# Last projection of a hybrid decoder block by seven products, with earlier x^T quarter loads, an ACT-freed retention bank and an earlier gated split

## The chip, the cores and the metric

One Trainium2 chip, one of its cores. The metric is device microseconds of one execution of the whole kernel (all of its inputs in HBM, the output written back to HBM). Its engines each run their own instructions in order: TensorE (PE, with its weight loads as PEld), VectorE (DVE), ScalarE (ACT), GpSimd (POOL) and SyncE (SP, which here only issues DMAs). Waits between engines are semaphores.

## The reference

One decoder layer on x of 512 tokens by 1024 channels, all in float32:

```
h = rms_norm(x, norm_pre);  proj = h @ w_in           # w_in: 1024 x 6936
o_a = nsa(...)        # compressed, selected and sliding-window attention, 8 heads
y_a = (o_a * silu(z_n)) @ w_nsa_o
o_b = retention(...)  # 4 heads, chunks of 128 tokens, group norm
y_b = (o_b * silu(z_r)) @ w_ret_o
merged = sigmoid(m_a) * y_a + sigmoid(m_b) * y_b
out = x + rms_norm(merged @ w_out, norm_post)         # w_out: 1024 x 1024
```

## The kernel before, in words

Every float32 product is made of three: each operand is split into a high part (rounded to the fp32r type, whose products PE takes at full rate) and a low part (the rest), and high x high, low x high and high x low are added up in a PSUM bank of 128 x 512. All matmuls go through `mm` (L230). The split of an operand is a copy for the high part, mostly by ACT (`act`, L197), and a subtraction for the low part by DVE (`sub_split`, which ends in `tt`, L209).

**Weights** come as a stream of 512 KB pieces. `load_next` (L356 for the plain ones, L359 for DRAM tiles) has SP load one into `raw` (4 buffers); each is split in two halves into `whi`/`wlo` (9 buffers each). One such half is the right-hand side or the weights of one k-tile. A buffer of `raw` is free when both halves are split, one of `whi`/`wlo` when PE has used it.

**The order of PE's work** is `main` (L1385) with the table `PLAN`: attention projections, then Z, MA 0, ZR 0, QK 0, VR 0, ZR 1, QK 1, VR 1, MB 0, NO 0, RO 0, MA 1, NO 1, MB 1, RO 1, and last `merged @ w_out`. Attention and retention are threaded between them. The program is written as coroutines; a planner (class `Order`) runs them at build time with a cost for each instruction and so fixes the order on every engine. A coroutine's priority is the second argument of `od.spawn` (a smaller number first), and `yield r, "act"` means "not before r, and when ACT's queue is short". What the planner thinks of time appears nowhere in this text; what matters is that each engine's order is fixed, so that an instruction that waits holds up all behind it.

**Seven products.** MA 1 and MB 1 already use a Winograd form: a 1024 x 512 projection is cut in quarters, and seven products of quarters stand in for eight (`seven`, L1219). Sums of weight quarters are made by DMAs in DRAM, issued by POOL: copies (L336) and accumulating DMAs (L338), all while attention runs (`weight_sums`). Sums of quarters of h^T are made by `h_sums`/`h_sum` (L1161, L1173): x^T is loaded again, scaled on ACT, added on DVE, split into the tiles `sums`.

**Places the change touches.**
- `ret` (L1013) ends a VR tile: ACT writes the high part of V from the bank, then DVE reads the same bank for the low part (`stt`, L222); only then is the accumulation bank free. PE's products go alternately to two such banks (`ACC`).
- `ret` also takes a reciprocal square root on POOL (`rv`, L209), for which DVE waits.
- `ga_split` (L1293) splits the gated attention output when all of retention is done; NO 0 needs it.
- `h_sums` waits for the same, then loads x^T; `tail_ya` (L1304) multiplies a bank of NO by its gate on DVE and frees the bank.
- `tail_yb` (L1311) ends a bank of RO: gate, sum with the NO part, split into `MO_H`/`MO_L`, the merged operand of the last projection.
- The last projection: two halves of 512 output channels, four token tiles t each, 8 k-tiles, three matmuls each. The last tile is done as two of 256 columns:

```
for half in range(2):
    for t in range(NT):
        n = 256 if half and t == NT - 1 else 512
        for j in range(512 // n):
            ps, e = yield from nat(...)          # 8 k-tiles x 3 matmuls of n columns
            od.spawn(tail_o(t, half + j, half * 512 + j * n, n, ps, e), 1)
```

- `tail_o` (L1327): ACT squares the bank with a running sum, DVE scales it by norm_post, POOL takes the root, DVE adds x, SP stores.

Of the kernel before, what the change touches and what calls it, by code (L numbers as in the profile page):

```python
# [39 lines left out]
HOLD = 1500.0  # L40
CAPS = (0, 4, 8, 11, 14, 16, 16, 16, 16)
# [98 lines left out]
def block_kernel(ctx: ExitStack, tc, x, xT, x0s, ws, small, w2s, norm_post, rope_r, dmask, out):  # L140
# [161 lines left out]
    XH = Ring([at(o, 512) for o in (28, 38, 40)])  # L302
# [11 lines left out]
    sums, atts = [], [0]  # L314
    mark = sp.tile([P, 1], FT, name="mark")
    for pieces in stream_shape():
        if pieces == "seven":
            b11, b12, b21, b22 = (ws[off + i * P * 1024:off + (i + 1) * P * 1024].rearrange("(p n) -> p n", p=P)
                                  for i in range(4))
            t1, t2, t3, t4 = (dp.tile([P, 1040], FT, name=f"t{len(sums)}{i}")[:, 0:1024] for i in range(4))  # L320
            sums.append(((t1, b11), (t3, b12), (t2, b11), (t4, b21), (t1, b12), (t3, b22), (t2, t3), (t4, t2)))
            loads.extend((a, [1024]) for a in (b11, b21, t2, t3, t1, t4, b22))
            off += 4 * P * 1024
            continue
        loads.append((off, pieces))
        off += P * sum(pieces)

# [46 lines left out]
    def splitter():  # L374
        for i, (_, pieces) in enumerate(loads):
            n = sum(pieces)
            for k in range(2):
                p = 2 * i + k
                own = KD <= p < 2 * KD
# [9 lines left out]
                if own:  # L389
# [621 lines left out]
    rr, dmr = [0.0], []  # L1011

    def ret(hp, t, ps, e):  # L1013
        yield od.need(*[f"att{i}{g}" for i in (2, 3) for g in range(2)])
        vh, vl = yield from VR[hp].get()
        yield e, "act"
        e = act(vh, ps, r=e, scale=rs(t))
        yield e, "dve"
        e = stt(vl, ps, rs(t), f(vh), OP.mult, OP.subtract, e)
        ACC.put(ps, e)  # L1020
# [45 lines left out]
        eo = e  # L1066
        if t < NT - 1:
# [19 lines left out]
        e = tt(rv, rv, nhalf[:, 2:4], OP.pow, e, "pool")  # L1087
        gb = yield from GB.get()
# [60 lines left out]
    def end_loads():  # L1149
        t = bp.tile([P, 28 * 256], FT, name="ends", tag="low")  # L1150
        XR.extend(t[:, o * 256:o * 256 + D] for o in (0, 4, 24, 0))
        OT.extend([*(t[:, o * 256:o * 256 + D] for o in (8, 12, 16)), at(28, D)])
        XR.append(t[:, 20 * 256:20 * 256 + D])
        for t in range(2):
            DMA.dma_start(XR[t], x[t * P:(t + 1) * P, :])
        DMA.dma_start(XR[2], x[2 * P:3 * P, :])
        DMA.dma_start(XR[4], norm_post.rearrange("(o n) -> o n", o=1).broadcast_to([P, D]))

    shr = [0.0] * 4

    def h_sums():  # L1161

        yield od.need("ga", *RETA)
        sum_tiles()
        for k in range(4):
            xs = []
            for i in range(2):
                xs.append((yield from XH.get()))
                DMA.dma_start(xs[i], xT[(4 * i + k) * P:(4 * i + k + 1) * P, :])
                e = od.dma(P * 2048, 0.0)  # L1170
            od.spawn(h_sum(k, xs, e), 1)

    def h_sum(k, xs, r):  # L1173
        yield r, "act"
# [8 lines left out]
        e0 = stt(tmp[0], tmp[2], -1.0, a11, OP.mult, OP.subtract, e2)  # L1183
        e1 = tt(tmp[1], a11, a21, OP.subtract, e)
# [47 lines left out]
    def seven_end(st, n, ps, e):  # L1232
# [10 lines left out]
        yield od.need(*[f"mg{k}" for k in range(4)])  # L1243
        if n == 3:
# [35 lines left out]
        rv = rsrow[:, i * 256:(i + 1) * 256].unsqueeze(1).broadcast_to([P, 2, 256])  # L1280
        e = stt(sg, sg, -1.0, rv, OP.mult, OP.mult, e) if j else tt(sg, sg, rv, OP.mult, e)
        yield e, "act"
        e = act(sg, sg, AF.Tanh, r=e, scale=0.5)
# [9 lines left out]
    def ga_split():  # L1293
        yield od.need(*RETA)
        for j in range(4):
            e = act(gah[:, j, :], szn[:, j, :])
            yield e, "pool"
            gar[0] = sub_split(gal[:, j, :], szn[:, j, :], gah[:, j, :], e)
        od.flags.add("ga")
# [11 lines left out]
    def tail_yb(half, ft, ps, e):  # L1311
# [4 lines left out]
        e = tt(sgs[ft], sgs[ft], sgs[4 + ft], OP.add, e)  # L1316
        yield e, "act"
        k = half * 4 + ft
        e = act(MO_H[k], sgs[ft], r=e)
        yield e, "dve"  # L1320
        mor[k] = sub_split(MO_L[k], sgs[ft], MO_H[k], e)
        od.flags.add(f"mg{k}")

    mor = [0.0] * 8
    ss2 = cp.tile([P, NT, 3], FT, name="ss2")

    def tail_o(t, i, c0, n, ps, e):  # L1327

        hc = slice(c0, c0 + n)
        end = c0 + n == D  # L1330
        sq = yield from NAT.get()
        yield e, "act"
        ea = act(sq[:, :n], ps[:, :n], AF.Square, r=e, scale=1.0 / 32.0, accum_out=ss2[:, t, i:i + 1])
        NAT.put(sq, ea)
        yield ea, "dve"
        if i:
            e = ts(ss2[:, t, i:i + 1], ss2[:, t, i:i + 1], ss2[:, t, i - 1:i], 4e-6 if i == 1 else 0.0,
                   OP.add, OP.add, ea)
        if end:
            r2 = sp.tile([P, 1], FT, name="rr", tag="rr", bufs=4)  # L1340
            er = tt(r2, ss2[:, t, i:i + 1], nhalf[:, 0:1], OP.pow, e, "pool")
        e = tt(OT[t][:, hc], ps[:, :n], XR[4][:, hc], OP.mult, ea)
        ACC.put(ps, e)
        if not end:
            return
        if t == NT - 1:
            yield od.need("xr3")
        yield er, "dve"
        e = er
        for a, b in ((0, 512), (512, D)) if t < NT - 1 else ((0, 384), (384, 768), (768, D)):  # L1350
            e = stt(OT[t][:, a:b], OT[t][:, a:b], r2, XR[t][:, a:b], OP.mult, OP.add, e)
            DMA.dma_start(out[t * P:(t + 1) * P, a:b], OT[t][:, a:b])
        if t == 0:
            DMA.dma_start(XR[3], x[3 * P:4 * P, :])
            od.flags.add("xr3")
# [29 lines left out]
    def main():  # L1385
# [60 lines left out]
        def merged(kt):  # L1446
            yield od.need(f"mg{kt}")
            yield mor[kt] + PE_LAG
        for half in range(2):
            blk = Block(8, 512)  # L1450
            for t in range(NT):
                c = slice(t * P, (t + 1) * P)
                n = 256 if half and t == NT - 1 else 512
                for j in range(512 // n):
                    ps, e = yield from nat(blk, t, n, t == NT - 1 and (j + 1) * n == 512,
                                           lambda kt: MO_H[kt][:, c], lambda kt: MO_L[kt][:, c], j * n, merged)
                    od.spawn(tail_o(t, half + j, half * 512 + j * n, n, ps, e), 1)
# [54 lines left out]
def stream_shape():  # L1512
# [7 lines left out]
    yield from [[1024]] * 8  # L1520


def stream(a):
# [28 lines left out]
    for half in range(2):  # L1552
        out += pair(w_out[:, half * 512:(half + 1) * 512])
# [34 lines left out]
```

## Time and profile before

| | |
|---|---|
| median of 3 runs | 527.37 us (527.1 to 527.5) |
| the profiled execution | 526.86 us |
| its span, first to last instruction | 525.1 us |
| TensorE clock granted, mean | 0.997 of full speed |
| PE busy | 514.8 us (98%), 2778 matmuls |
| DVE busy | 404.8 us (77%) |
| ACT busy | 291.9 us (56%) |
| POOL busy | 25.9 us (5%) |
| DMA | 68.87 MB, mean 131 GB/s |

The busy time of PE counts matmuls that overlap in the pipeline, so 98% says that nearly always one is in flight, not that they follow as closely as they could. How closely they follow is read from their starts, and where PE stood still from the list of its waits.

### The profile page before, as it was taken

The page shows a single profiled execution, that of the slowest core. Times are in us where ns is not written, and L with a number is a line of the kernel's source. Part 1 is how long each engine was busy: PE and PEld are TensorE (multiplying, and loading weights), DVE is VectorE, ACT ScalarE, POOL GpSimd, SP SyncE. Part 2 cuts the span into 40 slices and gives each one's busy share as a digit, 9 for nine tenths or more (in the row PEclk, how much of TensorE's full clock was granted, in tenths as well). Part 3 has the DMA queues.
Part 4 walks back from the last instruction along what each step waited for, and adds up shares of the span by engine and source line. Part 5 has one row for each costly group of instructions (what it writes and reads, how often), then busy time and mean ns, then how long its engine had stood idle before and what let it go on. Part 6 is the DMA issues. An engine that isn't in the chain of part 4 may idle for free.

```text
span 525.1 us, 7867 instructions
## 1 busy us (share of the span) xinstructions
PE 514.8 (98%) x2778; PEld 441.3 (84%) x2778; DVE 404.8 (77%) x980; ACT 291.9 (56%) x630; POOL 25.9 (5%) x56
## 2 busy tenths in 40 slices
PE   9999999999999999999999999999999999999995
PEld 7898888788888888888888888888788989988884
DVE  6798799989979799996876576787889867645533
ACT  6663799768568798763515253524557434323411
POOL 1000000000112011000000000000000000000000
PEclk9999999999999999999999999999999999999998
DMA  8941026501667338433131341131644726624032
GB/s 319 392 166 41 21 81 218 183 2 40 213 230 171 111 70 206 126 121 100 42 120 41 140 138 64 42 121 40 220 141 124 238 81 207 208 108 160 2 109 92
DMA packets 22456, 68.87 MB, mean 131 GB/s; under 512 B 2448, under 2 KB 3728, under 8 KB 22416
## 3 DMA queue, kind: packets, MB, share of 16 engines
q1 hardware_dynamic: 19968, 59.84, 32.8%
q0 software_dynamic: 2304, 8.39, 6.9%
q8 instruction: 22, 0.36, 0.3%
q14 instruction: 18, 0.15, 0.1%
q10 hardware_dynamic: 144, 0.14, 0.1%
HBM read 66.26 MB, written 10.49 MB: 146 GB/s over the span
## 4 chain that ended last, share of the span: by engine, by line
PE 81%; DVE 8%; DMA 5%; issue 2%; ACT 1%; SPq 1%; POOL 0%; POOLq 0%; DVEq 0%; ACTq 0%
PE bank L230 76%; PE bank L234 6%; DVE wlo L209 3%; DMA raw<-in_stream_dram 2%; DMA arena_l<-in_x_dram 2%; DVE arena_r L209 1%; DMA arena_l<-in_xT_dram 1%; DMA arena_f<-in_xT_dram 1%; DVE arena_l L846 1%; ACT arena_l L197 1%; DVE arena_l L218 1%; DVE arena_f L209 1%; SPq L479 0%; DVE nat L209 0%; SPq L356 0%
## 5 line engine op out<-in xcount | busy, mean ns | idle before, releaser
L209 DVE TENSOR_TENSOR wlo<-raw,whi 128x512 fp32r<-128x512 f32 x172 | 112.0, 687 | 6.8 <-ACT whi L197 5.7
L197 ACT ACTIVATE whi<-raw 128x512 fp32r<-128x512 f32 x157 | 94.5, 627 | 40.5 <-PE bank L230 33.5
L230 PE MATMUL bank<-whi,hTh 128*128 128x512 f32 x256 | 100.3, 407 | 0.6 <-DVE arena_r L222 0.5
L230 PE MATMUL bank<-whi,hTl 128*128 128x512 f32 x256 | 96.2, 391 | 0.0
L230 PE MATMUL bank<-wlo,hTh 128*128 128x512 f32 x256 | 96.1, 390 | 0.0
L230 PE MATMUL bank<-arena_r 128*128 128x256 f32 (+2 forms) x328 | 70.9, 336 | 0.3 <-DVE arena_r L209 0.3
L230 PE MATMUL bank<-arena_r,whi 128*128 128x512 f32 (+1 forms) x208 | 63.8, 382 | 1.0 <-DVE sg L222 1.0
L197 ACT ACTIVATE arena_l<-arena_l,stat 128x384 f32<-128x384 f32 (+3 forms) x109 | 57.8, 552 | 4.6 <-DVE stat L209 2.5
L197 ACT ACTIVATE arena_r<-bank 128x512 fp32r<-128x512 f32 (+2 forms) x80 | 45.1, 571 | 23.1 <-PE bank L234 21.5
L230 PEld LDWEIGHTS bank<-whi,hTl 128*128 128x128 f32 x256 | 48.1, 188 | 10.7
L230 PEld LDWEIGHTS bank<-whi,hTh 128*128 128x128 f32 x256 | 48.6, 190 | 9.7 <-DVE arena_r L222 0.9
L230 PEld LDWEIGHTS bank<-arena_r 128*128 128x128 f32 x328 | 51.1, 189 | 6.5 <-DVE arena_r L209 0.6
L209 DVE TENSOR_TENSOR arena_r<-bank,arena_r 128x512 fp32r<-128x512 f32 (+2 forms) x72 | 47.1, 657 | 10.9 <-ACT arena_r L197 10.4
L230 PEld LDWEIGHTS bank<-wlo,hTh 128*128 128x128 f32 x256 | 48.3, 188 | 8.2
L230 PE MATMUL bank<-hTh,whi 128*128 128x512 f32 (+1 forms) x144 | 52.4, 364 | 0.0
L230 PE MATMUL bank<-hTh,wlo 128*128 128x512 f32 (+1 forms) x144 | 51.2, 356 | 0.0
L230 PE MATMUL bank<-hTl,whi 128*128 128x512 f32 (+1 forms) x144 | 51.1, 355 | 0.0
L230 PE MATMUL bank<-whi,arena_r 128*128 128x512 f32 (+1 forms) x176 | 48.6, 352 | 0.0
L230 PEld LDWEIGHTS bank<-arena_r,whi 128*128 128x128 f32 x208 | 38.8, 188 | 8.8 <-DVE sg L222 1.6
L230 PE MATMUL bank<-arena_r,wlo 128*128 128x512 f32 x96 | 37.4, 389 | 0.0
L230 PEld LDWEIGHTS bank<-whi,arena_r 128*128 128x128 f32 x176 | 32.2, 189 | 4.6
L234 PE MATMUL bank<-ident,arena_l 128*128 128x128 f32 (+1 forms) x232 | 33.9, 273 | 0.9 <-DVE arena_l L566 0.9
(165 smaller groups left out, 771.0 us busy)
## 6 DMA issues: line engine op xcount, KB each, us to landing
raw<-in_stream_dram SPq DMA_DIRECT2D x77, 512.0 KB, 4.2
t<-in_stream_dram POOLq DMA_DIRECT2D x12, 512.0 KB, 5.4
raw<-t SPq DMA_DIRECT2D x8, 512.0 KB, 3.7
arena_f<-in_rope_r_dram SPq DMA_DIRECT2D x8, 256.0 KB, 2.6
t<-t POOLq DMA_DIRECT2D x4, 512.0 KB, 5.2
arena_f<-in_xT_dram SPq DMA_DIRECT2D x8, 256.0 KB, 3.7
ends<-in_x_dram SPq DMA_DIRECT2D x4, 512.0 KB, 5.4
arena_l<-in_xT_dram SPq DMA_DIRECT2D x7, 256.0 KB, 5.5
```

Of the source, the lines that this page charges most:

```text
L197: S.activation(o, i, func, **kw)
L209: (V if e == "dve" else G).tensor_tensor(o, a, b, op=op)
L218: V.tensor_scalar(o, a, s1, s2, op0=op0, op1=op1)
L230: T.matmul(ps, a, b, start=start, stop=stop)
L234: T.transpose(ps, a, idn)
L846: V.tensor_tensor_reduce(pv[:, b, :], sv[:, b, :], maskp[:, 512 - L:512], 1.0, -NEG, OP.add, OP.min, nm[:, b:b + 1])
```

## The change

The last projection is computed by seven products of quarters instead of tile by tile. With the merged operand cut into token halves and k halves A_ij (i the token half, j the k half) and w_out into b11, b12, b21, b22, seven products of 4 k-tiles x 2 token tiles x 3 matmuls of 512 columns are made, in the order of `plan`. Sums of weight quarters (t1 to t4) are made in DRAM by 16 more POOL DMAs (8 copies, 8 accumulating), issued in `ret` behind its `rv`: three in each of the first four `ret`, one in each of the last four (`OSUMS`). The stream's last part is 14 pieces of 512 KB instead of 8. Sums of quarters of the merged operand are made by `s_early` and `s_late` and split into `hTh`/`hTl`, which are free by then.

```
+OSUMS = (3, 3, 3, 3, 1, 1, 1, 1)
...
+        if pieces == "out":
...
+            for a, b in ((t1, b11), (t3, b12), (t2, b11), (t4, b21), (t1, b12), (t3, b22), (t2, t3), (t4, t2)):
+                osums.extend(zip(a, b))
+            loads.extend((a, [1024]) for q in (b11, t3, t2, t4, t1, b21, b22) for a in q)
...
+    def out_sums(n):
+        for _ in range(n):
+            i = len(oissued)
+            o, a = osums[i]
+            if i < 8:
+                G.dma_start(o, a)
+            else:
+                G.dma_start(o, a, accum_op=OP.add)
...
     def ret(hp, t, ps, e):
...
+        if t == NT - 1:
+            vf = yield from NAT.get()
+            yield e, "act"
+            e = act(vf, ps, r=e, scale=rs(t))
+            ACC.put(ps, e)
+            e = act(vh, vf, r=e)
+            yield e, "dve"
+            e = sub_split(vl, vf, vh, e)
...
         e = tt(rv, rv, nhalf[:, 2:4], OP.pow, e, "pool")
+        out_sums(OSUMS[4 * hp + t])
...
     def h_sums():
-        yield od.need("ga", *RETA)
-        sum_tiles()
+        yield od.need(*[f"qk1{t}" for t in range(NT)], *ATT)
         for k in range(4):
+            if k == 1:
+                yield od.need("ga", *RETA)
+                sum_tiles()
+                od.flags.add("sums")
...
-            od.spawn(h_sum(k, xs, e), 1)
+            od.spawn(h_sum(k, xs, e), 5)
...
     def ga_split():
-        yield od.need(*RETA)
+        es = []
         for j in range(4):
-            e = act(gah[:, j, :], szn[:, j, :])
-            yield e, "pool"
-            gar[0] = sub_split(gal[:, j, :], szn[:, j, :], gah[:, j, :], e)
+            yield od.need(f"qkend{j // 2}", *ATT)
+            yield qend[j // 2], "act"
+            es.append(act(gah[:, j, :], szn[:, j, :], r=qend[j // 2]))
+        for j in range(4):
+            yield od.need(f"qkend{2 + j // 2}")
+            yield max(es[j], qend[2 + j // 2]), "dve"
+            gar[0] = sub_split(gal[:, j, :], szn[:, j, :], gah[:, j, :], max(es[j], qend[2 + j // 2]))
...
+    def s_late(s, r):
+        yield r, "dve"
+        m0, m1, t = sgs[s], G1[s], sgs[4 + s]
+        e = tt(t[:, 0:256], m1[:, 256:512], m0[:, 256:512], OP.subtract, r)
+        e = stt(t[:, 256:512], t[:, 0:256], -1.0, m0[:, 0:256], OP.mult, OP.subtract, e)
+        es = e
+        yield e, "act"
+        sor[1][s] = yield from s_split(2 * s, slice(0, 512), t, e)
...
+        mor[4 + s] = yield from mo_split(4 + s, m1, 512, r)
...
+        e = stt(m0[:, 256:512], t[:, 256:512], -1.0, m1[:, 0:256], OP.mult, OP.subtract, es)
+        yield e, "act"
+        s4r[s] = e = yield from s_split(2 * s + 1, slice(256, 512), m0[:, 256:512], e)
...
+    def out_seven():
...
+        plan = ((X, quarter(0, 0)), (Q, summed(2)), (X, summed(1)), (Q, quarter(1, 1)), (X, summed(0)),
+                (Y, quarter(0, 1)), (X, summed(3)))
...
+            for ms in ((0, 1),) if n < 6 else ((0,), (1,)):
+                for s in range(4):
...
+                    for m in ms:
+                        lh, ll = of(s, m)
+                        for i, (a, b) in enumerate(((lh, wh), (ll, wh), (lh, wl))):
+                            T.matmul(ps[m], a, b, ...)
...
+                if n == 6:
+                    od.spawn(tail_o(ms[0], 1, ps[ms[0]], e), 1)
...
-        for half in range(2):
-            blk = Block(8, 512)
...
+        yield from out_seven()
```

X, Q and Y are pairs of PSUM banks. X is copied out by ACT after products 0 and 2, Q after product 1 (`keep`); `tail_o` adds such a copy on DVE (`plus`) before it squares. `s_early` makes the one sum that needs only the half of the merged operand that RO 0 gave. The last 8 halves of the stream go to places of their own in `arena_r`.

Where the order moves, on the engines of the prediction's steps (names as in the program; `bank_87` and `bank_88` are the two accumulation banks):

ACT, at the last VR tile of retention's first half (`ret`, t = 3; its bank is `bank_88`), before and then now:

```order
L197 ACTIVATE whi<-raw 128x512 x2
L197 ACTIVATE arena_l<-bank_89 128x256
L197 ACTIVATE arena_r<-bank_88,rs_127 128x512
L197 ACTIVATE arena_r<-bank_92 128x4x128
L197 ACTIVATE arena_l<-bank_87,rs_127 128x512
```

```order
L198 ACTIVATE whi<-raw 128x512 x2
L198 ACTIVATE arena_l<-bank_89 128x256
L198 ACTIVATE nat_113<-bank_88,rs_135 128x512
L198 ACTIVATE arena_r<-nat_113 128x512
L198 ACTIVATE arena_r<-bank_92 128x4x128
```

The bank is read by one ACT instruction, at the same place in the order as the old one; DVE's subtraction takes `nat_113` in place of the bank.

DVE at NO 0 (`sg<-sg,bank` is `tail_ya`; `nat<-arena_f` are the first sums of x^T quarters in `h_sum`), before and then now:

```order
L209 TENSOR_TENSOR wlo<-raw,whi 128x512 x5
L222 SCALAR_TENSOR_TENSOR sg<-sg,bank_87 128x512
L209 TENSOR_TENSOR nat_112<-arena_f 128x256
L222 SCALAR_TENSOR_TENSOR nat_113<-nat_112,arena_f 128x256
L209 TENSOR_TENSOR nat_113<-arena_f 128x256
L222 SCALAR_TENSOR_TENSOR nat_112<-nat_113,arena_f 128x256
L222 SCALAR_TENSOR_TENSOR sg<-sg,bank_88 128x512
```

```order
L210 TENSOR_TENSOR wlo<-raw,whi 128x512 x3
L223 SCALAR_TENSOR_TENSOR sg<-sg,bank_87 128x512
L210 TENSOR_TENSOR wlo<-raw,whi 128x512
L210 TENSOR_TENSOR nat_110<-arena_f,maskp 128x256
L223 SCALAR_TENSOR_TENSOR nat_111<-nat_110,maskp 128x256
L223 SCALAR_TENSOR_TENSOR sg<-sg,bank_88 128x512
L210 TENSOR_TENSOR nat_111<-maskp 128x256
L223 SCALAR_TENSOR_TENSOR nat_110<-nat_111,arena_f 128x256
L210 TENSOR_TENSOR sums<-nat_111,sums 128x256
L210 TENSOR_TENSOR nat_112<-arena_f 128x256
```

Two sums of 256 columns stand ahead of the second `tail_ya` instead of four, and they take the first x^T quarter pair, which SP now loads five pieces of the stream earlier, while retention runs. The second quarter pair (`nat_112<-arena_f`) is now loaded where the first one was.

DVE from the last bank of RO 1 on, now (before, the three rows of `tail_yb` and the weight splits stood there):

```order
L223 SCALAR_TENSOR_TENSOR arena_f<-arena_f,bank_88 128x512
L210 TENSOR_TENSOR arena_f<-arena_f 128x512
L210 TENSOR_TENSOR hTl<-sg,hTh 128x256
L210 TENSOR_TENSOR arena_f<-arena_f,sg 128x256
L223 SCALAR_TENSOR_TENSOR arena_f<-arena_f,sg 128x256
L210 TENSOR_TENSOR wlo<-raw,whi 128x512
L206 CAST whi<-raw 128x512
L210 TENSOR_TENSOR wlo<-raw,whi 128x512
L210 TENSOR_TENSOR hTl<-arena_f,hTh 128x512
```

The last row is what the third product's last k-tile needs of the merged operand.

## Rows read from the trace of the kernel before

**Rows 1.** The page's head and its first part: span; busy us (share) x instructions of each engine.
```profile
span 525.1 us, 7867 instructions
PE 514.8 (98%) x2778; PEld 441.3 (84%) x2778; DVE 404.8 (77%) x980; ACT 291.9 (56%) x630; POOL 25.9 (5%) x56
```

**Rows 2.** The waits of PE: its line <- engine and line waited for: us in total, times, longest.
```profile
PE bank L230 <- DVE sg L222: 1.0, 1, 1.0
...
PE bank L230 <- DVE arena_r L209: 0.5, 2, 0.3
PE bank L230 <- DVE arena_r L222: 0.5, 1, 0.5
```

**Rows 3.** The timeline of PE in the last projection: start us, us, engine, line, operation, out<-in, shapes, xcount. The first matmul; the last one of 512 columns, merged with the first one of 256; the last.
```profile
474.84 0.39 PE L230 MATMUL bank<-whi,arena_r 128*128 128x512 f32 x1
...
512.69 0.50 PE L230 MATMUL bank<-whi,arena_r 128*128 128x512 f32 x2
...
518.55 0.28 PE L230 MATMUL bank<-whi,arena_r 128*128 128x256 f32 x1
```

**Rows 4.** The timelines of PE, DVE and ACT at the end of VR 0; in brackets the idle time before, and its releaser.
```profile
267.89 0.50 PE L230 MATMUL bank<-whi,hTh 128*128 128x512 f32 x1 [0.46 <-DVE arena_r L222]
264.49 1.89 DVE L209 TENSOR_TENSOR wlo<-raw,whi 128x512 fp32r<-128x512 f32 x3
267.09 0.75 DVE L222 SCALAR_TENSOR_TENSOR arena_r<-bank,rs,arena_r 128x512 fp32r<-128x512 f32 x1
261.82 0.68 ACT L197 ACTIVATE arena_r<-bank,rs 128x512 fp32r<-128x512 f32 x1
```

**Rows 5.** The timelines of PE, DVE, ACT and SP at NO 0.
```profile
377.22 0.73 PE L230 MATMUL bank<-arena_r,whi 128*128 128x512 f32 x2 [1.00 <-DVE sg L222]
372.47 0.69 DVE L222 SCALAR_TENSOR_TENSOR sg<-sg,bank 128x512 f32<-128x512 f32 x1
375.01 0.43 DVE L209 TENSOR_TENSOR nat<-arena_f 128x256 f32<-128x256 f32 x1 [1.86 <-ACT arena_f L197]
376.49 0.68 DVE L222 SCALAR_TENSOR_TENSOR sg<-sg,bank 128x512 f32<-128x512 f32 x1
372.37 0.73 ACT L197 ACTIVATE arena_f<-arena_f,x 128x512 f32<-128x512 f32 x1 [2.16 <-DMA arena_f<-in_xT_dram]
374.26 0.72 ACT L197 ACTIVATE arena_f<-arena_f,x 128x512 f32<-128x512 f32 x1 [1.16 <-DMA arena_f<-in_xT_dram]
368.79 1.38 SPq L1169 DMA_DIRECT2D arena_f<-in_xT_dram  x3
```

**Rows 6.** The timelines of ACT, DVE, POOL and SP at the end: the last tile of 512 columns that ends a row of the output, then the last tile of 256.
```profile
513.18 0.60 ACT L197 ACTIVATE nat<-bank 128x512 f32<-128x512 f32 x1 [4.75 <-PE bank L230]
514.03 0.68 DVE L209 TENSOR_TENSOR ends<-bank,ends 128x512 f32<-128x512 f32 x1
514.77 1.42 DVE L222 SCALAR_TENSOR_TENSOR ends<-ends,rr 128x512 f32<-128x512 f32 x2
518.92 0.38 ACT L197 ACTIVATE nat<-bank 128x256 f32<-128x256 f32 x1 [2.40 <-issue]
519.72 0.54 POOL L209 TENSOR_TENSOR rr<-ss,nhalf 128x1 f32<-128x1 f32 x1 [4.99 <-DVE ss L218]
520.30 1.54 DVE L222 SCALAR_TENSOR_TENSOR arena_f<-arena_f,rr,ends 128x384 f32<-128x384 f32 x3 [0.33 <-POOL rr L209]
520.94 1.36 SPq L1352 DMA_DIRECT2D out_dram<-arena_f  x3
```

**Rows 7.** Busy time by stretch (from:to, us, then busy us and count of PE, PEld, DVE, ACT, POOL, granted clock, DMA share, GB/s): RO 1, then the last projection. Then DVE's low and high parts of weights in both stretches together (count | busy us, mean ns), a run of such splits in the timeline, and a split that waits for ACT's high part.
```profile
453.05:474.85 21.80, 21.80 (x99) 18.04 (x98) 11.76 (x19) 6.74 (x11) 0.00 (x0) 1.00 0.47 169
474.85:518.90 44.05, 43.98 (x217) 37.24 (x215) 18.70 (x32) 10.97 (x25) 1.64 (x3) 1.00 0.25 84
L209 DVE TENSOR_TENSOR wlo<-raw,whi 128x512 fp32r<-128x512 f32 x17 | 11.2, 688 | 0.0
...
L205 DVE CAST whi<-raw 128x512 fp32r<-128x512 f32 x1 | 0.4, 422 | 0.0
...
369.46 3.09 DVE L209 TENSOR_TENSOR wlo<-raw,whi 128x512 fp32r<-128x512 f32 x5
460.83 0.69 DVE L209 TENSOR_TENSOR arena_r<-sg,arena_r 128x512 fp32r<-128x512 f32 x1 [0.70 <-ACT arena_r L197]
```

**Rows 8.** The timeline of POOL: DMAs of the weight sums that are there already (L336 copies, L338 accumulating), then the first and the last of the four roots of retention's first half.
```profile
139.50 1.80 POOL L336 DMA_DIRECT2D t<-in_stream_dram  x3
144.07 0.52 POOL L336 DMA_DIRECT2D t<-in_stream_dram  x1 [2.78 <-DVE arena_l L209]
158.28 0.84 POOL L338 DMA_DIRECT2D t<-in_stream_dram  x1 [0.40 <-issue]
163.95 0.84 POOL L338 DMA_DIRECT2D t<-in_stream_dram  x1 [4.82 <-issue]
247.66 0.73 POOL L209 TENSOR_TENSOR rv<-rv,nhalf 128x2 f32<-128x2 f32 x1 [12.48 <-DVE rv L216]
...
283.30 0.70 POOL L209 TENSOR_TENSOR rv<-rv,nhalf 128x2 f32<-128x2 f32 x1 [10.30 <-DVE rv L216]
```

**Rows 9.** The tile `raw` from 225 us on: time from issue to landing; and SP's issues of the last pieces of RO 1 and the first of the last projection.
```profile
DMA to landing us min/median/max: 3.0/3.9/5.6
434.42 20.48 SPq L356 DMA_DIRECT2D raw<-in_stream_dram  x8
```

More of the change, by code (lines that the diff above doesn't have):

```diff
@@ L378, in splitter @@
                 p = 2 * i + k
-                own = KD <= p < 2 * KD
+                late = p - 2 * len(loads) + 8
+                own = KD <= p < 2 * KD or late >= 0
+                if late >= 0:
+                    yield od.need("gb")
                 yield lambda: own or in_ring(p) < in_ring(len(done)) + NW
@@ L1243, in seven_end @@
         yield od.need(*[f"mg{k}" for k in range(4)])
+        if not st["off"]:
+            yield od.need("sh3")
         if n == 3:
@@ new lines, in block_kernel, with keep, tail_o @@
+    s4r = [0.0] * 4
+    mor = [0.0] * 8
+    G1.extend([maskp, at(28, 512), at(38, 512), at(40, 512)])
+    ss2 = cp.tile([P, NT, 2], FT, name="ss2")
+    p1, p7 = [], []
+    def keep(ps, lst, e, dst=None):
+        if dst is None:
+            dst = yield from NAT.get()
+        else:
+            yield od.need("s42", "s43")
+        yield e, "act"
+        e = act(dst, ps, r=e)
+        lst.append((dst, e))
+    def tail_o(t, i, ps, e, plus=None):
+        hc = slice(i * 512, (i + 1) * 512)
+        o = OT[t][:, hc]
+        if plus:
+            yield lambda: len(plus[0]) > plus[1]
+            b, r = plus[0][plus[1]]
+            yield max(e, r), "dve"
+            e = tt(o, ps, b, OP.add, max(e, r))
+            free[t, i] = e
+            src = o
+        else:
+            src = ps
+        yield e, "act"
+        ea = act(rsrow, src, AF.Square, r=e, scale=1.0 / 32.0, accum_out=ss2[:, t, i:i + 1])
@@ L1343, in tail_o @@
-        ACC.put(ps, e)
-        if not end:
+            er = tt(r2, ss2[:, t, 1:2], nhalf[:, 0:1], OP.pow, e, "pool")
+            od.flags.add(f"pow{t}")
+        tt(o, src, XR[4][:, hc], OP.mult, ea)
+        if not i:
             return
-        if t == NT - 1:
-            yield od.need("xr3")
         yield er, "dve"
         e = er
-        for a, b in ((0, 512), (512, D)) if t < NT - 1 else ((0, 384), (384, 768), (768, D)):
+        if t > 1:
+            yield lambda: len(parts) == 2 * len(loads)
@@ L1444, in main @@
                 od.spawn(h_sums(), 1)
-        def merged(kt):
-            yield od.need(f"mg{kt}")
-            yield mor[kt] + PE_LAG
-        for half in range(2):
-            blk = Block(8, 512)
[L1451 to L1457, printed above, removed]
+        od.flags.add("gb")
+        yield from out_seven()
     hook[0] = [lambda: load_xT(1), lambda: load_xT(2)]
@@ L1519, in stream_shape @@
         yield from ["seven"] if b in SEVEN else [[1024]] * (2 if b[0] == "NO" else 4)
-    yield from [[1024]] * 8
+    yield "out"
 def stream(a):
@@ L1551, in stream @@
         out += block(name, i)
-    for half in range(2):
-        out += pair(w_out[:, half * 512:(half + 1) * 512])
+    out += [a for r in range(2) for c in range(2) for a in pair(w_out[r * 512:(r + 1) * 512, c * 512:(c + 1) * 512])]
     return np.concatenate([o.reshape(-1) for o in out])
```

197 lines of the change are left out of this document (154 added, 43 removed).

## The prediction

> **What bounds the kernel now.** I read the page's head and first part first: PE is busy in 514.8 of 525.1 us [rows 1], so a change pays if it takes matmuls away or closes one of PE's waits, and it costs if PE has to wait for something new. Next the list of PE's waits: behind the start-up only a few are left, and two of them belong to places that the change touches, 1.0 us for DVE's `tail_ya` and 0.5 us for DVE's low part of V [rows 2]. Then the timeline of the last projection. PE starts it at 474.84 and its last matmul, at 518.55, takes 0.28, so it ends at 518.83; the windows show a granted clock of 1.00 throughout and DVE, ACT and DMA far from full [rows 3, 7]. What is left after 518.83 is a chain ACT, DVE, POOL, DVE, SP and the landing, 525.1 - 518.8 = 6.3 us.
>
> **Matmuls.** Before: eight tiles of 8 k-tiles x 3 matmuls, seven of them 512 columns wide (168 matmuls) and the last one as 48 matmuls of 256. Now: 7 products x 4 k-tiles x 2 token tiles x 3 = 168 matmuls of 512. So the 48 narrow ones go and nothing wide comes. The first 168 took from 474.84 to the start of the first narrow one; with the pair at 512.69 the second starts at 512.69 + (512.69 - 474.84)/167 = 512.92, a pace of 0.2266 us. The new last matmul would start at 512.69 and end 0.39 later, at 513.08 instead of 518.83 [rows 3]. **-5.75 us**, if PE keeps its pace.
>
> **The bank of V.** PE's 0.46 us wait at 267.89 ends with DVE's read of the bank, from 267.09 to 267.84; that read stood behind a run of weight splits (three of them from 264.49), while ACT had read the same bank at 261.82 [rows 4]. Now only ACT reads it, at the same place in its order, and the bank is free at 262.5, almost 5 us before PE asks. What it adds, 0.6 us of ACT for a second copy, lies in an engine that is not waited for there. **-0.46 us.** The same edit in the second half meets no wait.
>
> **x^T and the gated split.** At NO 0 PE waits 1.00 us for a `tail_ya` that DVE runs at 376.49. Ahead of it DVE stood still for 1.86 us, up to 375.01, for ACT, which scaled x^T at 372.37 and 374.26, after waiting 2.16 and 1.16 us for loads that SP issued at 368.79 [rows 5]. Now the second `tail_ya` stands behind only two sums of 256 columns, and their x^T is loaded five pieces of the stream sooner; a piece feeds 24 matmuls here, 5.4 us, so that is some 27 us. The pair that SP now issues near 368.8 feeds sums ahead of the third `tail_ya`: these would start near 375.0 + 0.4, and the third bank is not full before 376.1 (the last of its matmuls ends where the wait at 377.22 began). So what is late next, is late for nobody. The gated split, 4 ACT and 4 DVE instructions, moves forward by the same number; nothing is added. **-1.0 us.**
>
> **DVE and ACT in RO 1 and the last projection.** This is where covers must hold. DVE is busy 11.76 + 18.70 = 30.5 us there now [rows 7]. Added: 12 weight splits at 0.69 = 8.3; 4 high parts that go to DVE at 0.42 = 1.7 [rows 7]; 24 sums and low parts of 256 columns at 0.43 [rows 5] and 4 low parts of 512 at 0.69 = 13.1; 6 additions of a saved bank at 0.69 = 4.1. Together 27.2, so 57.7 us in PE's 21.8 + 38.2 = 60.0. In a run, five splits took 3.09, so 0.60 each and not 0.69 [rows 7], which makes it some 50, five sixths. It fits as a sum; the question is the order. After RO 1's last bank the order has nine rows down to the low part that the third product's last k-tile needs: 4 x 0.69 + 0.42 x 4 + 0.69 = 5.1 us, with a backlog of about 2 and an ACT round trip of 0.7 [rows 7] some 8 us. PE has two products and three quarters of a third ahead of that, 66 matmuls or 15 us. The third product's own weights come after a dozen rows more, about 9 us against 10.9. The tightest margin is thus near 2 us, and I take **0** for waits here, with 0 and 6.1 us as ends (the upper one below).
>
> **DMA.** 14 pieces of 512 KB in place of 8. A piece now feeds 12 matmuls, 2.7 us; it lands 3.9 us after issue (at most 5.6), four are in flight, and the first four are issued long before, by 455 [rows 9]. Cover: three pieces, 8 us. The two pairs of x rows and norm_post are the same loads as before. The DRAM sums are issued in retention, with RO 0, MA 1, NO 1 and MB 1 between them and their loading. **0**; gone, the cover would cost up to 1.7 us once (5.6 - 3.9).
>
> **The tail.** Before, the last tile is 256 wide: from ACT's start at 518.92 to DVE's last additions at 520.30 it takes 1.38. Now it is 512 wide, and the second half of another row of tiles has its addition put in front. In the 512-wide tile DVE's scaling starts 0.85 after ACT (513.18 to 514.03) and takes about 0.6 of the queue; the extra addition takes 0.7 (1.42 for two), and POOL's root, ready before, no longer matters: 0.85 + 0.6 + 0.7 = 2.15 [rows 6]. **+0.8 us**; at least 0.2 (only the wider square, 0.60 - 0.38), at most 1.25 with one more issue of SP in the way (1.36/3).
>
> **Sum.** -5.75 - 0.46 - 1.0 + 0.8 = -6.4. The profiled execution took 526.86, of which 525.1 span; that makes 520.45. The median of the runs is 0.51 higher, so **521.0 us**. With the bounds of the tail alone 520.4 to 521.4. A measurement here tells about 0.2% from no change, 1.05 us.
>
> **Rivals.**
> *A wait inside the last projection.* DVE becomes the bound: 57.7 us of single durations and 12 low parts that each stand still 0.7 for ACT [rows 7] make 57.7 + 8.4 = 66.1 against 60.0 if nothing fills the gaps: 6.1 us at the worst, 527.1; half of it is likelier, 524.1. For it: five sixths full and every sum a chain over two engines. Against it: the order puts splits between the links, and PE has two products in hand. Chance 0.14.
>
> *The two waits are refilled.* x^T, gate splits and ACT copies keep DVE and ACT as full as before near 267 and 376, so another instruction stands in front and the 1.46 us stay: 522.4. For it: before 267 DVE ran splits without a gap [rows 4], and the work of none of these edits is less than before. Against it: both instructions that PE waits for have lost what stood ahead of them. Chance 0.13.
>
> *POOL is late.* The 16 DMAs stand on POOL between the roots that DVE waits for, three behind each of the first. Three copies were issued in 1.80 us, but an accumulating DMA was held back 4.82 and took 0.84 [rows 8]. If each of the three were held so, a group would take 17.0 us with its root 17.7; the four roots lie within 283.30 - 247.66 = 35.6, three gaps, and would need 53: 17.5 us late, DVE's queue with them, 538. It decides from 6.4 + 1.1 = 7.5 us of lateness on. Against it: the first three groups hold eight copies and one accumulating DMA, and the row of three copies. Chance 0.04, slower.
> The Trainium skill, "SBUF — State Buffer", section "SBUF: two separate sides", states a mechanism for this rival: POOL cannot write descriptors while DVE runs certain copies, and such a DMA took about 3100 ns instead of 620. By that figure three issues would be an estimated 9.3 us, with one hold 14.1 against a gap of 11.9, some 2 us late and 523. The trace does not bear it out: with DVE busy 77% of the span [rows 1], a copy took 0.52 or 0.6 to issue and an accumulating DMA 0.84; the time went by between the issues [rows 8].
>
> *The change does not do what it says:* excluded for the matmuls, since the order shows 168 wide ones and no narrow one.
>
> **Chances and range.** Forecast 0.69, refilled waits 0.13, a wait in the projection 0.14, POOL 0.04. The forecast's own range, with 0.5 for what differs between executions, is 519.9 to 521.9; refilled waits reach 522.9; half of the DVE rival lies below 524.1. So 519.9 to 523.6. Faster by more than 0.2% (below 526.3): all but POOL and the top of the DVE rival, 0.94; within: 0.02; slower: 0.04.
>
> **What would show it.** Right: 168 matmuls of 512 columns at 0.227 us, 38.2 us from the first to the end of the last; PE's waits without the two; DVE's extra addition ahead of the last three; about 7.1 us from PE's end to the span's. Wrong: a wait of PE for DVE or ACT in the second or third product, a POOL root that starts later after its DVE input than now, raw pieces on which ACT waits.

## The result and the profile after

520.33 us (median of 4 runs, 519.61 to 521.05) against 527.24 of the kernel before beside it: a ratio of 0.987 (95% interval 0.985 to 0.989). The forecast was 521.0 (519.9 to 523.6), faster.

The profiled execution is the slowest of the four, 521.05. I cut it at four marks of PE that both kernels have: the last start of an `arena_r,vcs` matmul (the attention's end), the first matmul of NO 0, the first and the last of the last projection. The same cuts in all later runs make the table that the rest hangs on (us; the last column is the median of the runs):

| kernel | to the attention's end | then to NO 0 | NO 0 to the projection | projection, first to last start | from there to the end | median |
|---|---|---|---|---|---|---|
| before | 218.25 | 149.60 | 106.99 | 43.71 | 6.55 | 527.24 |
| after | 219.99 | 148.59 | 105.66 | 37.85 | 7.21 | 520.33 |
| v_undone | 218.32 | 149.45 | 105.66 | 37.85 | 7.22 | 520.93 |
| x_undone | 218.94 | 148.69 | 108.49 | 37.85 | 7.13 | 522.93 |
| seven_only | 218.50 | 149.59 | 108.16 | 37.86 | 7.19 | 523.23 |
| early_only | 218.94 | 148.57 | 105.67 | 43.71 | 6.51 | 524.96 |
| load_early_prio1 | 218.80 | 148.57 | 105.66 | 37.85 | 7.22 | 519.85 |
| split_late | 218.09 | 148.72 | 106.55 | 37.85 | 7.89 | 521.12 |
| no_sums | 219.86 | 148.58 | 105.67 | 37.85 | 7.14 | 520.74 |
| pool_one_gap | 218.57 | 186.91 | 105.66 | 37.85 | 7.21 | 558.01 |
| swap | 219.27 | 148.59 | 105.66 | 43.00 | 7.18 | 524.99 |
| tail_unheld | 218.69 | 148.57 | 105.66 | 37.85 | 7.13 | 520.41 |
| tail_y_first | 218.76 | 148.59 | 105.65 | 37.86 | 6.54 | 519.26 |
| best | 218.18 | 148.58 | 105.66 | 37.86 | 6.52 | 519.32 |

From before to after: +1.74, -1.01, -1.33, -5.86, +0.66, which is -5.8, the difference of the spans (525.1 and 519.3). The last stretch is worked out from spans given to 0.1 us, so it is good to about 0.05, and differences below that say nothing.

The page of after, its span and first part, against [rows 1]: PE has 2730 records for 2778, DVE and ACT more work, and PE is still the bound.
```profile
span 519.3 us, 7888 instructions
...
PE 508.1 (98%) x2730; PEld 435.6 (84%) x2730; DVE 425.9 (82%) x1031; ACT 306.6 (59%) x660; POOL 38.5 (7%) x72
```
The waits of PE in after (columns as in [rows 2]): the waits for DVE's `tail_ya` and for the low part of V are gone. The first line is new, and lies near 33 us, where nothing was changed.
```profile
PE bank L235 <- DVE arena_f L593: 1.8, 1, 1.8
PE bank L1669 <- DVE rsrow L248: 1.0, 1, 1.0
PE bank L235 <- DVE arena_l L593: 0.9, 1, 0.9
PE bank L231 <- DVE arena_r L210: 0.3, 1, 0.3
```
**The last projection.** The windows of RO 1 and of the projection in after (columns as in [rows 7]), then PE's last matmul.
```profile
452.45:474.24 21.79, 21.79 (x99) 18.04 (x97) 18.66 (x37) 10.39 (x20) 0.00 (x0) 1.00 0.42 145
474.24:512.48 38.24, 38.24 (x169) 31.38 (x167) 33.29 (x61) 19.94 (x42) 2.41 (x3) 1.00 0.51 179
```
```profile
512.09 0.39 PE L1538 MATMUL bank<-arena_r,hTh 128*128 128x512 f32 x1
```
PE is busy in all of the 38.24 us, at a granted clock of 1.00: 43.99 before, so -5.75, the forecast's figure. DVE works 18.66 + 33.29 = 51.95 us in the two stretches, where single durations had given 57.7 and the pace of runs some 50.

**The V bank.** Timeline of PE at the end of VR 0, before (beside [rows 4]) and after:
```profile
267.04 0.39 PE L230 MATMUL bank<-whi,hTl 128*128 128x512 f32 x1
...
268.23 0.40 PE L230 MATMUL bank<-wlo,hTh 128*128 128x512 f32 x1
...
268.69 2.45 PE L230 MATMUL bank<-arena_r 128*128 128x256 f32 x18
270.98 0.40 PE L230 MATMUL bank<-whi,hTh 128*128 128x512 f32 x1
```
```profile
268.79 0.39 PE L231 MATMUL bank<-whi,hTl 128*128 128x512 f32 x1
...
269.69 2.31 PE L231 MATMUL bank<-arena_r 128*128 128x256 f32 x18
271.84 0.40 PE L231 MATMUL bank<-whi,hTh 128*128 128x512 f32 x1
```
Four wide matmuls and the 18 of retention take 270.98 - 267.04 = 3.94 before and 271.84 - 268.79 = 3.05 after. The wait that the trace gives as 0.46 cost 0.89: 0.62 from start to start (267.04 to 267.89, less a pace of 0.23), since the idle time is counted from the end of a matmul of 0.39 and the next one would have started 0.23 after it; then 0.34 instead of 0.23 for the first one behind the wait, and 2.29 instead of 2.15 for the 18.

**NO 0.** DVE and SP in after, to be held against [rows 5]:
```profile
371.97 0.68 DVE L223 SCALAR_TENSOR_TENSOR sg<-sg,bank 128x512 f32<-128x512 f32 x1
...
373.17 0.42 DVE L210 TENSOR_TENSOR nat<-arena_f,maskp 128x256 f32<-128x256 f32 x1
373.63 0.43 DVE L223 SCALAR_TENSOR_TENSOR nat<-nat,maskp 128x256 f32<-128x256 f32 x1
374.24 0.69 DVE L223 SCALAR_TENSOR_TENSOR sg<-sg,bank 128x512 f32<-128x512 f32 x1 [0.19 <-PE bank L231]
```
```profile
338.61 0.42 SPq L1215 DMA_DIRECT2D maskp<-in_xT_dram  x1
...
368.86 0.90 SPq L1215 DMA_DIRECT2D arena_f<-in_xT_dram  x2
```
The second `tail_ya` stands behind two sums, as the order said, starts 2.25 us sooner than before, though NO 0 begins 0.73 later, and waits for PE, not PE for it. The first pair was issued at 338.6, 30 us ahead of the second.

**POOL** in after, against [rows 8]: three copies, then accumulating DMAs, the last one between two chained tiles.
```profile
250.10 1.64 POOL L344 DMA_DIRECT2D o<-in_stream_dram  x3
...
277.97 0.87 POOL L346 DMA_DIRECT2D o<-in_stream_dram  x1 [3.03 <-issue]
284.17 0.71 POOL L210 TENSOR_TENSOR rv<-rv,nhalf 128x2 f32<-128x2 f32 x1 [5.33 <-DVE rv L217]
...
299.38 0.82 POOL L346 DMA_DIRECT2D o<-in_stream_dram  x1 [7.94 <-issue]
326.57 0.71 POOL L210 TENSOR_TENSOR rv<-rv,nhalf 128x2 f32<-128x2 f32 x1 [26.37 <-DVE rv L217]
```
Every root waits for DVE, none for a DMA. But the third group (two copies and one accumulating DMA) was done only 5.3 us ahead of the next root; the fourth, three accumulating ones, took 284.86 to 300.2, and had 26 us to spare.

### The profile page after: what moved, and what is told of

Same layout as the page of the kernel before. It is cut to its first block, busy times and chain, and to the rows that moved or that the text cites. A ratio compares the mean times of both kernels' runs of the same rounds, so it can differ in the third digit from the quotient of the medians.

```text
span 519.3 us, 7888 instructions
## 1 busy us (share of the span) xinstructions
PE 508.1 (98%) x2730; PEld 435.6 (84%) x2730; DVE 425.9 (82%) x1031; ACT 306.6 (59%) x660; POOL 38.5 (7%) x72
## 4 chain that ended last, share of the span: by engine, by line
PE 85%; DVE 7%; DMA 6%; issue 1%; ACT 1%; SPq 0%; DVEq 0%; ACTq 0%
PE bank L231 72%; PE bank L1538 7%; PE bank L235 6%; DMA raw<-in_stream_dram 4%; DVE wlo L210 2%; DMA arena_l<-in_xT_dram 1%; DVE arena_r L210 1%; DVE arena_l L873 1%; DVE arena_l L219 1%; DVE arena_f L210 1%; ACT arena_l L198 0%; DVE nat L210 0%; DVE ends L223 0%; SPq L506 0%; DVE arena_f L593 0%
## 5 line engine op out<-in xcount | busy, mean ns | idle before, releaser
L198 ACT ACTIVATE whi<-raw 128x512 fp32r<-128x512 f32 x160 | 96.7, 627 | 45.7 <-PE bank L231 32.3
L210 DVE TENSOR_TENSOR wlo<-raw,whi 128x512 fp32r<-128x512 f32 x176 | 114.9, 685 | 8.6 <-ACT whi L198 7.9
L235 PEld LDWEIGHTS bank<-ident,arena_l 128*128 128x128 f32 (+1 forms) x232 | 27.9, 138 | 6.7 <-DVE arena_l L593 1.1
L873 DVE CUSTOM_DVE_ANT_0 arena_l<-bank,maskp 128x512 f32<-128x512 f32 (+3 forms) x64 | 29.3, 485 | 3.2 <-PE bank L231 2.9
```

The costliest lines, as they stand in the source:

```text
L198: S.activation(o, i, func, **kw)
L210: (V if e == "dve" else G).tensor_tensor(o, a, b, op=op)
L235: T.transpose(ps, a, idn)
L873: V.tensor_tensor_reduce(pv[:, b, :], sv[:, b, :], maskp[:, 512 - L:512], 1.0, -NEG, OP.add, OP.min, nm[:, b:b + 1])
```

## The experiments

**Parts alone.** Edits: in `v_undone` the branch `if t == NT - 1` of `ret` is taken out; in `x_undone` the x^T sums and `ga_split` are the old code (the first pair still in `maskp` and `at(28, 512)`); `seven_only` is both; `early_only` is the kernel before with both edits put in. Lines of x_undone:
```diff
-            od.spawn(h_sum(k, xs, e), 5)
+            od.spawn(h_sum(k, xs, e), 1)
...
-        es = []
+        yield od.need(*RETA)
         for j in range(4):
-            yield od.need(f"qkend{j // 2}", *ATT)
```


> The changed kernel with the V bank's edit taken back: ACT's high part and DVE's low part both read the bank again, in both halves of retention. My theory: the wait of PE for DVE's read comes back, 0.46 us by the kernel before, so about 520.8 (520.3 + 0.46); up to 521.2 if the 0.87 us that the trace gained between 166 and 341 us hang on it as a whole. Rival, the gain in that stretch came from the new order of the planner or from the execution, not from this read: 520.3 and no wait of PE for that tile.

> The changed kernel with the first x^T pair loaded, and the gated output split, only behind all of retention, and the sums at their old priority. My theory: DVE stands still for ACT in NO 0 again and PE waits 1.0 us for the second bank of NO 0, so 521.3; up to 521.7 if the 1.33 us that the trace gained there hang on it. Rival, the new projection's work already keeps that bank free in time: 520.3.

> The seven products and the new tail alone, both early edits taken back. My theory: -5.75 + 0.58 for matmuls and tail against the kernel before, so 527.2 - 5.2 = 522.0; the two waits of PE are there. Rival, the early edits are worth nothing by themselves: 520.3. Rival, the new DVE and ACT work needs the early edits as cover: above 523, with PE waiting inside the last projection.

> The kernel before with the early edits alone (V bank by ACT, first x^T pair early and with least priority, gated output split sooner), the last projection and the tail as before. My theory: 527.2 - 0.46 - 1.0 = 525.8, down to 525.0 by the 0.87 and 1.33 us that the trace of the changed kernel gained there. Rival, the two waits come back at another instruction: 527.2. All four profiles also show the first 40 us, whose instructions are the same in all kernels: if the 1.8 us wait of PE near 33 us in the profiled run of the changed kernel is a matter of the execution, some of these runs have it and others don't.

The V edit is worth 0.9 to 1.0 us in the second column, wherever it is put in or taken out (149.60, 149.45, 149.59 without, 148.57 to 148.72 with); the wait of 0.46 is back in v_undone:
```profile
267.94 0.50 PE L231 MATMUL bank<-whi,hTh 128*128 128x512 f32 x1 [0.46 <-DVE arena_r L223]
```
The early x^T and split are worth 1.32 on the kernel before, and 2.5 to 2.8 on the new one: x_undone shows two waits where the kernel before had one.
```profile
380.06 0.73 PE L231 MATMUL bank<-arena_r,whi 128*128 128x512 f32 x2 [1.25 <-DVE sg L223]
...
386.66 0.50 PE L231 MATMUL bank<-arena_r,whi 128*128 128x512 f32 x1 [0.87 <-DVE sg L223]
```
So my 522.0 for seven_only and 521.3 for x_undone were 1.2 and 1.6 us too low. Part of that comes from how I undid the edit: with four tiles for x^T in place of three the second pair is there at once, and nine sums and low parts stand on DVE ahead of the third `tail_ya`, four before. The seven products alone bring -5.85 and +0.6 in the last two columns, with the early edits or without.

**Which of the early edits.**
```diff
-            od.spawn(h_sum(k, xs, e), 5)
+            od.spawn(h_sum(k, xs, e), 1)
```


> The changed kernel with the first x^T pair loaded as early, but its sums at the old priority, ahead of the weight splits: seven sums and low parts and two weight splits stand on DVE ahead of the second bank's instruction in NO 0, in place of two sums. Theory that the priority is what counts: DVE reaches that bank near 376.2 and not at 374.2, and PE waits there or at the next bank by 0.3 to 1.3 us, 520.6 to 521.6. Theory that the early load alone counts: no wait of PE in NO 0, 520.3.

In `split_late`, `ga_split` alone is the old code.

> The changed kernel with the gated output split only behind all of retention, as in the kernel before; the first x^T pair stays early and its sums at least priority. Theory that the early x^T is what closed the wait in NO 0 (the run with old priority still had none): no wait there, NO 0 to the last projection in 105.7 us, 520.3. Theory that the earlier split is what matters: its four ACT and four DVE instructions (4 x 0.6 on each) run into the first bank of NO 0, PE waits 0.5 to 1.5 us, 520.8 to 521.8.

The priority is worth nothing here (105.66, no wait of PE for `sg`): my reckoning of 0.3 to 1.3 was wrong. The second `tail_ya` started 6.8 us into NO 0 (374.17), 1.1 later than in after, and was still done before its bank was asked for, three banks or 8.2 us in. In the new kernel the split is worth 0.89, as the second theory had it and against the first: PE waits once for the first `tail_ya`.
```profile
373.03 0.73 PE L231 MATMUL bank<-arena_r,whi 128*128 128x512 f32 x2 [0.62 <-DVE sg L223]
```
What the early load is worth by itself was not run. x_undone and split_late, which both split late, differ by 1.94 (108.49 and 106.55): the early load with the order of its sums, and with it the flaw of x_undone named above. The 7.89 in the last column of split_late goes back to a piece of the weight that ACT took at 493.38, 20.0 us into the projection, where in after it was 18.2: DVE's queue behind it lay later against PE, and its last sum of squares came 1.93 us after the last matmul's start instead of 1.21; see the tail.

**POOL.**
```diff
-OSUMS = (3, 3, 3, 3, 1, 1, 1, 1)
+OSUMS = (16, 0, 0, 0, 0, 0, 0, 0)
```


> The changed kernel with all sixteen weight-sum DMAs issued behind the first root of retention, none behind the others. The trace of the changed kernel shows eight accumulating DMAs at 0.82 to 0.88 each, held back by 3.0, 4.9 and 7.9 us where one follows another, and copies at 0.55. Theory that POOL's queue can hold up the roots: 8 x 0.55 + 8 x 0.85 + seven holds of 3.0 to 7.9 make 32 to 66 us against 9.4 us between the first two roots; the second root comes 20 us or more late, DVE's queue with it, PE waits, and the time is 535 to 570. Theory that only the issue counts: 4.4 + 6.8 = 11.2, 1.8 us late, which DVE and PE hardly see: 520.3 to 522.

> The changed kernel without the sixteen DMAs of the weight sums: the products load plain quarters of the weight in their place, so the sums are left out of the computation. My theory, that these DMAs cost nothing where they stand: 520.3, the last projection at 38.2 us. Rival: they cost something by DVE's waits behind POOL or by traffic beside the stream, and the time falls by 0.3 to 1.5 us, to 518.8 to 520.0.

Timelines of POOL and DVE with all sixteen in one gap, and PE's longest wait there:
```profile
267.48 0.87 POOL L346 DMA_DIRECT2D o<-in_stream_dram  x1 [6.74 <-issue]
272.86 0.83 POOL L346 DMA_DIRECT2D o<-in_stream_dram  x1 [4.52 <-issue]
...
305.59 0.82 POOL L346 DMA_DIRECT2D o<-o  x1 [4.61 <-issue]
306.14 1.02 POOL L210 TENSOR_TENSOR rv<-rv,nhalf 128x2 f32<-128x2 f32 x1
```
```profile
307.20 1.00 DVE L219 TENSOR_SCALAR arena_l<-bank,mv,rv 128x256 f32<-128x256 f32 x2 [36.93 <-POOL rv L210]
```
```profile
PE bank L235 <- DVE arena_l L210: 35.2, 1, 35.2
```
The rival's mechanism is real: each accumulating DMA is held 4.5 to 6.7 us, the second root comes 58 us behind the first and not 9.4, DVE stands still 36.9 us for it, and 558.0 is 38 us more than after. The stretch grew by 38.3 for 35.2 of listed wait: when PE went on at 309.45, its granted clock was 0.50, the lower of its two levels (1.2 GHz and not 2.4), until about 315.4, and its matmuls started 0.43 apart instead of 0.23.
```profile
312.00:315.00 3.00, 3.00 (x8) 2.31 (x7) 0.25 (x1) 0.00 (x0) 0.00 (x0) 0.50 0.00 0
```
In after this did not happen because the groups of three stand where copies are cheap or the next root is far. Without the sixteen (no_sums) nothing is gained: 520.74, and the same stretches.

The Trainium skill, "SBUF — State Buffer", section "SBUF: two separate sides", says that a POOL DMA which overlaps certain copies of DVE takes about 3100 ns instead of 620. No issue was that long here, with DVE busy 82% of the span: three copies took 1.64, an accumulating one 0.82 to 0.88. But DVE's busy share is no test of that rule, in the prediction either: in none of the fourteen profiles does one of DVE's copies (CAST, COPY) run beside a POOL DMA's issue, so no run here shows that case. What holds POOL is the time between two issues, which that rule doesn't speak of.

**The cover in the projection.**
```diff
-        plan = ((X, quarter(0, 0)), (Q, summed(2)), (X, summed(1)), ...
+        plan = ((X, quarter(0, 0)), (X, summed(1)), (Q, summed(2)), ...
```
The start flags stayed with the places, so here the second product replaces the first one's banks and the third adds to what a bank held; instructions, operands and waits are otherwise as meant.

> The changed kernel with the second and third product exchanged (their weights too): the product whose operands RO 1's last bank makes now follows the first at once. In the changed kernel's trace the low part of its last k-tile is done at 480.6 and used near 489.2; here it would be used near 483.8, still 3 us later. Theory that the order has a margin of about 8 us there: no wait for low parts; but the product adds to the first one's banks, and ACT must have copied those (done 0.7 to 1.5 us after they are full, nothing between now), so PE waits 0.5 to 1.5 us for ACT, 520.8 to 521.8. Theory that DVE's chain is tight, as the rival of a wait in the projection says: PE waits over 3 us for hTl in the second product, 523 or more.

PE, then ACT, then the windows (columns as in [rows 7]) around the second wait:
```profile
479.98 0.50 PE L1538 MATMUL bank<-whi,hTh 128*128 128x512 f32 x1 [0.86 <-ACT nat L198]
...
493.24 0.73 PE L1538 MATMUL bank<-whi,arena_r 128*128 128x512 f32 x2 [2.08 <-ACT nat L198]
```
```profile
492.07 0.63 ACT L198 ACTIVATE arena_r<-raw 128x512 fp32r<-128x512 f32 x1 [1.83 <-DMA raw<-in_stream_dram]
492.60 1.06 ACT L198 ACTIVATE nat<-bank 128x512 f32<-128x512 f32 x2
```
```profile
493.00:494.00 1.00, 0.77 (x3) 0.67 (x4) 1.00 (x3) 1.00 (x3) 0.00 (x0) 1.00 0.40 160
494.00:495.00 1.00, 1.00 (x4) 0.78 (x3) 0.71 (x3) 1.00 (x3) 0.00 (x0) 0.54 0.88 233
495.00:496.00 1.00, 1.00 (x4) 0.81 (x3) 1.00 (x3) 0.23 (x1) 0.00 (x0) 0.50 0.72 287
496.00:497.00 1.00, 1.00 (x4) 0.72 (x4) 1.00 (x3) 0.28 (x1) 0.00 (x0) 0.50 0.07 20
```
525.0 is what the theory of the tight chain gave, but there is no wait for a low part: DVE's chain is not tight. The first wait is the one expected. I had not seen the second: the copy of the next pair of banks stands on ACT behind a weight split whose piece had not landed, and no product lies between any more. And the 2.08 us cost more than themselves: soon after PE goes on, the granted clock is at 0.50, the lower level, for some 3 us. The stretch grew by 5.15 for 2.94 of listed waits: from start to start the two waits cost 1.0 and 2.2, and the nine matmuls between 494.04 and 497.68 lost 1.6 at the lower clock.

**The tail.** `tail_unheld` takes away the hold of row 0; `tail_y_first` also puts row 3's additions behind those that take the sixth product's banks; `best` adds the old priority of the sums.
```diff
         if t > 1:
             yield lambda: len(parts) == 2 * len(loads)
+        if t == 3:
+            yield lambda: (0, 0) in free and (1, 0) in free
...
-            if t == 0 and a:
-                yield od.need("pow1")
```


> The changed kernel, in which the second half's addition of the row of tiles 0 no longer waits for the root of row 1, and so stands on DVE ahead of the last sum of squares. My theory of the tail: that addition (0.6 of DVE's queue) lies on the path behind the last root, and DVE has a hole of 0.55 us ahead of the last sum of squares in which it fits, so the stretch from the last matmul's end to the span's end goes from 6.8 to 6.2 to 6.3 us and the time to 519.8. Rival: SP's queue of stores or their landing sets the end and not DVE's additions, so the stretch stays at 6.8 and the time at 520.3. Rival: the addition misses the hole and holds up the last sum of squares, 0.1 to 0.6 more.

> The changed kernel with two edits in the order of its end: the row of tiles 0 adds its second half without waiting for the root of row 1, and row 3 adds its two halves only behind the additions that take the last but one product's banks. Theory that DVE's queue over the last 15 us sets the end, where it stands still 0.45 and 0.25 us for POOL and ACT: those holes are filled, the first rows' additions are done ahead of the last sum of squares, and from the last matmul's start to the span's end it takes 6.5 to 6.7 instead of 7.1 to 7.2 us; 519.7. Rival, stores set the end: 7.1 to 7.2, 520.3.

> The end of the run before in this group (row 0 unheld, row 3 behind) and the x^T sums at the old priority, which gave no wait of PE and a median of 519.85. Theory that both add up: 519.3 to 519.6. Theory that the priority made no difference and its median lay within the spread of the start-up: 519.7, as the run with the end alone.

DVE over the last 13 us, first in after, then in tail_y_first:
```profile
506.79 1.42 DVE L223 SCALAR_TENSOR_TENSOR ends<-ends,rr 128x512 f32<-128x512 f32 x2 [0.45 <-POOL rr L210]
508.12 1.28 DVE L210 TENSOR_TENSOR ends<-bank,nat 128x512 f32<-128x512 f32 x2
509.66 1.45 DVE L210 TENSOR_TENSOR ends<-ends 128x512 f32<-128x512 f32 x2 [0.25 <-ACT rsrow L198]
...
513.30 0.21 DVE L219 TENSOR_SCALAR ss<-ss 128x1 f32<-128x1 f32 x1 [0.55 <-ACT rsrow L198]
...
514.02 2.19 DVE L223 SCALAR_TENSOR_TENSOR ends<-ends,rr,arena_f 128x512 f32<-128x512 f32 x4
```
```profile
505.70 1.28 DVE L210 TENSOR_TENSOR ends<-bank,nat 128x512 f32<-128x512 f32 x2
506.90 1.40 DVE L223 SCALAR_TENSOR_TENSOR ends<-ends,rr 128x512 f32<-128x512 f32 x2
...
512.06 0.21 DVE L219 TENSOR_SCALAR ss<-ss 128x1 f32<-128x1 f32 x1 [0.37 <-ACT rsrow L198]
512.93 1.54 DVE L223 SCALAR_TENSOR_TENSOR ends<-ends,rr,arena_f 128x384 f32<-128x384 f32 x3
```
In after the four instructions at 514.02 are row 0's addition and the three that end the run. Unheld alone, row 0 brought nothing: in that run DVE's whole queue lay 0.6 us later against PE, the hole was gone, and the last sum of squares came 1.88 us after the last matmul's start instead of 1.21. With row 3 moved, both holes of 0.45 and 0.25 are filled, row 0 is done ahead, and the stretch falls from 7.21 to 6.54, back to that of the kernel before. 519.26 us (ratio to before 0.9855, 0.9842 to 0.9867) is the best of all kernels here; by times alone it can't be told from after (the intervals overlap), by the tail it can. `best` reads the same, so its last part adds nothing.

## Why the prediction was right, and where it was off

- **Matmuls, -5.75:** measured -5.75, and the same in every run with the seven products in the planned order.
- **V bank, -0.46:** right mechanism (the wait came back in v_undone), but half the size: it was worth 0.9 to 1.0. I took the idle time that the trace lists for the price; start to start it was 0.62, and PE's first instructions behind it were slower by another 0.25.
- **x^T and the split, -1.0:** -1.33. The same fault for 0.15 (375.84 to 377.22, less one pace, is 1.15), and the pair of matmuls behind the wait lost 0.1 more. That the split added no work was right; that it got no share of the gain was wrong for the new kernel, where split_late puts 0.89 on it. The third bank was full at 376.2 and not 376.1, which changes nothing.
- **DVE and ACT in the projection, 0:** right. The "tightest margin near 2 us" was that of the third product's own weights; it came out at 3.1: the first low part was done at 482.5 (the first of the two at 481.80) and used at 485.57. For the sums 15 us against 8 were forecast; the last low part for the third product was done at 480.60 and used near 489.2, a margin of 8.6. For ACT the step was too hopeful: swap shows that a product between a bank's end and its next use is what hides ACT's copy, since one late piece of the weight holds ACT's queue. DVE in after:
```profile
479.92 0.68 DVE L210 TENSOR_TENSOR hTl<-arena_f,hTh 128x512 fp32r<-128x512 f32 x1
...
481.80 1.29 DVE L210 TENSOR_TENSOR wlo<-raw,whi 128x512 fp32r<-128x512 f32 x2
```
- **DMA, 0:** right for PE. But a piece took 4.4 us in the median and 7.2 at most from issue to landing, where the step had 3.9 and 5.6, and ACT waited for pieces by 5.8 us in all. The prediction had named such waits as a sign of being wrong; they came, and PE did not wait. What was missing at the end came out in DVE's queue and the tail (split_late).
- **Tail, +0.8:** +0.55 from the last matmul's end (6.27 before, 6.82 after). The extra addition lies where I put it. What I did not see is that DVE's queue of the last 13 us, with its waits for POOL and ACT, decides, and so that the order of the additions of rows 0 and 3 gives 0.67 back. Row 3's part of that was not run without row 0's.
- **The sum, -6.4:** the stages give -1.01 - 1.33 - 5.75 + 0.55 = -7.54. The start-up took away 1.74 in the profiled run, and the medians differ by 6.9. So that 521.0 came within 0.7 of 520.33 is in part luck: the waits and the tail were worth 1.1 more than forecast, the start-up hid it, and the 0.51 added for the median went the other way (the profiled run was the slowest).
- **Rivals:** no wait in the projection. The two waits were not refilled; but x_undone shows how it goes: the third and fourth `tail_ya` are late, and PE waits 2.1 us for them. POOL was not late; the mechanism holds, and the margin was 5.3 us at the third group.

The start-up's difference is not the change's: up to the attention's end PE, DVE, ACT and POOL have the same instructions in the same order in all fourteen kernels (1178 of PE, 548 of DVE), and yet the first column runs from 218.09 to 219.99. ACT, in before and after:
```profile
27.76 0.64 ACT L197 ACTIVATE whi<-raw 128x512 fp32r<-128x512 f32 x1 [0.48 <-DMA raw<-in_stream_dram]
```
```profile
29.43 0.64 ACT L198 ACTIVATE whi<-raw 128x512 fp32r<-128x512 f32 x1 [0.89 <-DMA raw<-in_stream_dram]
```
The piece of the weight lands 1.67 us later, and the wait of 1.8 us near 33 us follows. The same wait was 1.3 us in early_only, 1.8 in no_sums and absent in tail_unheld. Why it lands late in some executions stays open.

## What to carry to other kernels

Price a wait of the bounding engine from start to start of its instructions, not by the idle time listed, and add what the first instructions behind it lose. Read a rival that did not happen by its margin: three accumulating DMAs cost nothing in a gap of 42 us, and sixteen DMAs in one of 9.4 cost 38. Where a narrow last tile is given up, look at the whole queue of the engine that closes the program: its holes, filled with work that stood behind them, paid back the tail.

## What had not been expected of the hardware

A stop of PE of 2.08 us inside a stretch at full clock was followed by some 3 us at a granted clock of 0.50 (swap, 494 to 497), and behind a stop of 35.2 us PE had 0.50 for 6 us (pool_one_gap); stops of 0.46 to 1.25 us in v_undone and x_undone left it at 1.00 right after. On POOL a queue of accumulating DMAs goes on at one per 5.4 us (267.48 to 305.59 for eight), though each takes 0.83 to issue, and of the eight copies ahead of them the first three took 1.63 us, while the other five began 1.0 to 2.3 us apart after a pause of 2.98.
